# Split-float products in a Trainium2 decoder layer: the three passes of two products dealt out alternately

## The chip, the cores and the metric

The kernel runs on one core of one Trainium2 chip. The metric is the device time of one launch in microseconds (us); three runs before the change give a median of 1633.29 us (1633.14 to 1633.54). The engines are named as in the profile: PE (TensorE, matrix products; PEld is its weight load), DVE (VectorE), ACT (ScalarE), POOL (GpSimd), SP (SyncE, which issues most DMAs).

## The reference

One decoder layer on x of 1024 rows (sequence) by 1024 columns, all in float32:

```
def hybrid_mixer(h, lower_bound, w_in, conv_w, ..., w_out):
    proj = h @ w_in                                   # 1024 x 8192
    xa, ga, q, f, v, g, m_a, m_b = jnp.split(proj, SPLIT_POINTS, axis=-1)
    xa = causal_depthwise_conv(xa, conv_w, conv_b)
    y_a = rg_lru(xa, w_r, b_r, w_i, b_i, lam) * jax.nn.gelu(ga)
    ...
    o = rms_norm(hgrn2_chunkwise(qf, kf, log_f, vf), hg_norm)
    y_b = o * jax.nn.silu(g)
    y = jax.nn.sigmoid(m_a) * y_a + jax.nn.sigmoid(m_b) * y_b
    return y @ w_out

x = x + hybrid_mixer(rms_norm(x, norm_mix), ...)
h = rms_norm(x, norm_mlp)
x = x + jnp.square(jax.nn.relu(h @ w_up)) @ w_down    # 1024 x 4096 hidden
return rms_norm(x, norm_final)
```

`rg_lru` has two gate products per 256-column block (`w_r`, `w_i`) and a linear recurrence along the sequence; `hgrn2_chunkwise` is gated linear attention with 8 heads of 128.

## The kernel before

**Split products.** PE works on float32r operands, so each float32 operand is kept as a high part and a rest (`split`, L75: ACT casts the high part, L76; DVE subtracts, L77). A product is then three passes that add up in one PSUM bank: high x low, high x high, low x high (`mm3`, L113 to L117). L115, L116 and L117 in the profile are these passes; the output's name tells the product. Of the eight PSUM banks four have the tag `pj`, two `sc`, two `hg` (L59).

**Mixing stage** (two chunks c of 512 rows, four head pairs p each; L626 to L645). For every pair: `project_v` (L282) makes v with the rows as output partitions, four row tiles one after the other, each in a bank of its own and copied out by ACT (L293). `project` (L270) makes one of xa, q, f, g, mb, ga, ma: two output tiles `pp[0]` and `pp[1]` of 128 x 512 in two `pj` banks, eight contraction tiles, and for each contraction tile the three passes of `pp[0]` and then those of `pp[1]`: 48 matmuls. `rg_lru` (L326) has for each half s of the pair's channels two gate banks, `pr` (six matmuls) and then `pi` (six); ACT makes sigmoids and a tanh of them (L337 to L340), DVE a reciprocal (L345), some products and the scan (L352). Its tiles `rw`, `ri` and `rr` have one buffer each. `hgrn` (L381) is a chain on DVE: products with decays (`mul`, L384), and between them five blocks of small score matmuls on PE (`sc`: three at L394, one at L479, one at L497) that need q x f, qa, qb and kk from DVE. `gates` (L561) projects g, mb, ga, ma; DVE multiplies with `pj_g` straight out of its banks (L566), then merges g with the sigmoid of mb (L571).

**Output projection**: chunk 0 in `out_proj` (L599: four row tiles in four banks), chunk 1 inside the second norm's loop (L714 to L736: two row tiles at a time, then adds on DVE and the norm of those rows).

**MLP**, one level of a Strassen-like scheme. In the up projection (`hidden`, L804) each step fills one bank. In the down projection (L936 to L971), eight blocks kb take two quads `qs` each, and for two row tiles `pr` of a half the seven steps of `PLAN` run: for each `pr` six matmuls (three per quad) into the bank (X, Y or Z; X goes on accumulating while DVE has read its partial sum), then for each `pr` one DVE add into `x2` (L963). The first quad's tiles come from pools on the left side, the second's from pools opened with `side="right"` (L880 to L901). In the last half of the last block the row tiles run one after the other (`alone`).

**Order.** The program is written in the order above, but a scheduler of the framework orders each engine's instructions by readiness and priority (`rg_lru` and the weight splits run at raised priority), so the gate products stand inside f, the score blocks inside g, mb and ga, and the splits of coming weights anywhere on ACT and DVE. Weights come through four raw buffers (DMA from SP) and six `w` buffers, that is three tiles of high and rest (L79 to L92).

Of the kernel before, what the change touches and what calls it, by code (L numbers as in the profile page):

```python
# [18 lines left out]
P = 128  # L19
# [13 lines left out]
QUADS = 16  # L33
# [8 lines left out]
def trunk(ctx: ExitStack, tc: tile.TileContext, x, wts, mlp, pv, gains, mask_f, mask_u, out):  # L42
# [66 lines left out]
    def next_w():  # L109
        used[0] += 1  # L110
        return get_w(used[0] - 1)

    def mm3(o, ah, al, bh, bl, first, last, goes_on=False):  # L113
        how = {"skip_group_check": True} if goes_on else {}
        PE.matmul(o, ah, bl, start=first, stop=False, **how)  # L115
        PE.matmul(o, ah, bh, start=False, stop=False, **how)  # L116
        PE.matmul(o, al, bh, start=False, stop=last, **how)  # L117


    ident = const.tile([P, P], F32, tag="ident", name="ident")  # L120
# [149 lines left out]
    def project(c, name):  # L270

        pp = [bank("pj", f"pj_{name}_{s}") for s in range(2)]
        for half in range(2):
            wh, wl = next_w()
            for k in range(4):
                hh, hl = kt(hT[c], 4 * half + k)
                for s in range(2):
                    cols = slice(k * 256 + s * P, k * 256 + (s + 1) * P)
                    mm3(pp[s], wh[:, cols], wl[:, cols], hh, hl, half == 0 and k == 0, half == 1 and k == 3)
        return pp  # L280

    def project_v(c, name):  # L282
        v = mt("v", f"v_{name}", (P, 4, 256))
        w = [next_w(), next_w()]
        for tt in range(4):
            pp = bank("pj", f"pv_{name}_{tt}")
            for k in range(8):
                hh, hl = kt(hT[c], k)
                cut = slice(tt * P, (tt + 1) * P)
                cols = slice((k % 4) * 256, (k % 4 + 1) * 256)  # L290
                wh, wl = w[k // 4]
                mm3(pp[:, :256], hh[:, cut], hl[:, cut], wh[:, cols], wl[:, cols], k == 0, k == 7)
            A.copy(v[:, tt, :], pp[:, :256])  # L293
        return v

    def conv(c, p, pp):
# [29 lines left out]
    def rg_lru(c, p, xc, xh, xl):  # L326
        wh, wl = next_w()
        hs = mt("h", f"h{c}{p}", (P, 2, T))
        for s in range(2):
            u = 2 * p + s  # L330
            pr, pi = bank("pj", f"pr{c}{u}"), bank("pj", f"pi{c}{u}")
            for o, k0 in ((pr, 0), (pi, 2)):
                for k in range(2):
                    cols = slice((k0 + k) * 256 + s * P, (k0 + k) * 256 + (s + 1) * P)
                    mm3(o, wh[:, cols], wl[:, cols], xh[:, k, :], xl[:, k, :], k == 0, k == 1)
            w = mt("rw", f"rw{c}{u}")
            A.activation(w, pr, AF.Sigmoid, bias=pvt[:, PV_BR + u : PV_BR + u + 1])  # L337
            A.activation(w, w, AF.Tanh, scale=sp4[:, u : u + 1])
# [260 lines left out]
    def out_proj(c, ys, res, done, between=lambda: None):  # L599
        for hf in range(2):  # L600
            pp = [bank("pj", f"po{c}{hf}{tt}") for tt in range(4)]
            for j in range(4):
                wh, wl = next_w()
                for k in range(2):
                    ku = 2 * j + k
                    yh, yl = kt(ys, ku)
                    cols = slice(k * 512, (k + 1) * 512)
                    for tt in range(4):
                        cut = slice(tt * P, (tt + 1) * P)
# [16 lines left out]
    for c in range(NC):  # L626
# [4 lines left out]
            out_proj(0, ys, res0, done0, lambda: first_norm(1))  # L631
        ys = a2_set(a2y, f"y{c}")
        for p in range(NPAIR):
            v = project_v(c, f"{c}{p}")
# [79 lines left out]
    for part in range(2):  # L714
# [5 lines left out]
        for hf in range(2):  # L720
            pp = {tt: bank("pj", f"po1{hf}{tt}") for tt in tts}
            for j in range(4):
                wh, wl = next_w()
                for k in range(2):
                    ku = 2 * j + k
                    yh, yl = kt(ys, ku)
                    cols = slice(k * 512, (k + 1) * 512)
                    for tt in tts:
                        cut = slice(tt * P, (tt + 1) * P)
                        mm3(pp[tt], yh[:, cut], yl[:, cut], wh[:, cols], wl[:, cols], ku == 0, ku == 7)  # L730
# [11 lines left out]
    ops_w, raw_q = {}, {}  # L742
# [193 lines left out]
    for kb in range(n_kb):  # L936
        last = kb + 1 == n_kb
        qs = order[2 * kb : 2 * kb + 2]
        for half in range(2):
# [109 lines left out]
```

## Time and profile before

| what | value |
|---|---|
| median of three runs | 1633.29 us |
| profiled execution, span from first to last instruction | 1630.3 us |
| PE busy | 1585.8 us (97%), 9240 matmuls |
| DVE busy | 1211.9 us (74%) |
| ACT busy | 762.2 us (47%) |
| mean granted TensorE clock | 0.996 of full speed |
| mixing stage of a pair | about 107 us; up projection about 320 us; down projection about 310 us |

The span is that of the profiled execution itself; what a run takes beyond it lies before the first and after the last instruction. In a group or timeline row stand the line, the engine, the operation, output<-inputs, shapes, and busy time; brackets hold the idle time of the engine just ahead of it and what ended it. Matmuls are pipelined: a row's duration is longer than the distance to the next row, so the pace of PE is read from starts.

### The profile page before, as it was taken

Reading aid. Unit: us, or ns where it says so; the run is one execution under the profiler, and the core shown is the slowest. Engines: PE = TensorE matmul, PEld = TensorE weight load, DVE = VectorE, ACT = ScalarE, POOL = GpSimd, SP = SyncE. Lnnn points to the kernel's source line nnn. Section 1 sums busy time; section 2 is a strip of 40 time slices with the busy share of each in tenths; the row PEclk is TensorE's granted clock in tenths of the full one; section 3 lists DMA queues with packets and bytes.
Section 4 is the critical chain, followed back from the end, with each engine's and each line's share of the span. In section 5 each row is a group of like instructions: output and inputs, shape, how many; then the busy total and the mean of one; then the engine's idle time right before and its main releaser. Section 6 shows DMA issues by size and latency. Waiting matters only on the chain.

```text
span 1630.3 us, 23190 instructions
## 1 busy us (share of the span) xinstructions
PE 1585.8 (97%) x9240; PEld 1303.6 (80%) x9240; DVE 1211.9 (74%) x1751; ACT 762.2 (47%) x1186; POOL 62.8 (4%) x99
## 2 busy tenths in 40 slices
PE   7999999999999999999999998999999999999998
PEld 6788788788788788788787876888888878888886
DVE  5975956848764965848759688977777888888876
ACT  4643545435442544436435566767766732221113
POOL 0010100100100000000100000000000000000000
PEclk9999999999999999999999998999999999999999
DMA  6222223223244222222222352666666566666652
GB/s 236 91 66 91 91 66 103 66 91 93 78 165 142 80 77 91 78 84 98 66 91 91 125 200 102 262 247 239 233 248 247 216 259 237 238 246 249 252 207 104
DMA packets 57996, 246.51 MB, mean 151 GB/s; under 512 B 6688, under 2 KB 6816, under 8 KB 47136
## 3 DMA queue, kind: packets, MB, share of 16 engines
q1 hardware_dynamic: 56304, 239.27, 40.8%
q10 hardware_dynamic: 1584, 5.77, 1.0%
q8 instruction: 72, 1.18, 0.3%
q14 instruction: 36, 0.29, 0.1%
HBM read 185.24 MB, written 59.77 MB: 150 GB/s over the span
## 4 chain that ended last, share of the span: by engine, by line
PE 82%; DVE 15%; issue 1%; ACT 1%; DMA 1%; POOL 0%; DVEq 0%; POOLq 0%; SPq 0%; ACTq 0%
PE dX L115 4%; PE dX L117 4%; PE dX L116 4%; PE uX L115 3%; PE uX L117 3%; PE uX L116 3%; DVE wL L77 2%; PE pj_ga L117 2%; PE pj_ga L116 2%; PE pj_ga L115 2%; PE pj_ma L117 2%; PE pv L116 2%; PE pv L115 2%; PE pj_ma L116 2%; PE pv L117 2%; PE pj_f L117 2%
## 5 line engine op out<-in xcount | busy, mean ns | idle before, releaser
L77 DVE TENSOR_TENSOR wL<-raw,wH 128x1024 fp32r<-128x1024 f32 x160 | 194.4, 1215 | 151.3 <-ACT wH L76 148.7
L76 ACT CAST wH<-raw 128x1024 fp32r<-128x1024 f32 x160 | 167.9, 1050 | 166.9 <-issue 67.1
L963 DVE TENSOR_TENSOR acc<-acc,dX 128x512 f32<-128x512 f32 x128 | 86.7, 682 | 29.6 <-PE dX L117 28.9
L76 ACT CAST wA<-q 128x512 fp32r<-128x512 f32 x32 | 19.8, 621 | 130.9 <-PE dX L117 82.8
L963 DVE TENSOR_TENSOR acc<-acc,dY 128x512 f32<-128x512 f32 x64 | 43.6, 683 | 16.6 <-PE dY L117 14.9
L345 DVE RECIPROCAL rr<-rr 128x512 f32<-128x512 f32 x16 | 53.5, 3345 | 0.0
L823 ACT ACTIVATE b<-b 128x512 f32<-128x512 f32 x48 | 30.2, 631 | 38.7 <-DVE b L822 38.6
L115 PE MATMUL pv<-wL,hT0H 128*128 128x256 f32 x128 | 37.1, 289 | 0.0
L117 PE MATMUL pv<-wH,hT0L 128*128 128x256 f32 x128 | 36.7, 286 | 0.0
L116 PE MATMUL pv<-wH,hT0H 128*128 128x256 f32 x128 | 36.6, 286 | 0.0
L115 PE MATMUL pv<-wL,hT1H 128*128 128x256 f32 x128 | 36.5, 285 | 0.0
L116 PE MATMUL pv<-wH,hT1H 128*128 128x256 f32 x128 | 36.2, 283 | 0.0
L117 PE MATMUL pv<-wH,hT1L 128*128 128x256 f32 x128 | 36.2, 283 | 0.0
L311 DVE SCALAR_TENSOR_TENSOR xc<-xp,pvt,xc 128x512 f32<-128x512 f32 x48 | 33.1, 746 | 0.0
L551 ACT ACTIVATE on<-po 128x128 f32<-128x128 f32 x64 | 17.0, 278 | 33.5 <-PE po L541 33.2
L570 ACT ACTIVATE smb<-pj_mb 128x512 f32<-128x512 f32 x16 | 9.6, 597 | 45.4 <-PE pj_mb L117 45.2
L824 ACT ACTIVATE b<-b 128x512 f32<-128x512 f32 x48 | 30.0, 629 | 1.1
L384 DVE TENSOR_TENSOR seg<-seg 128x128 f32<-128x128 f32 (+2 forms) x96 | 26.8, 309 | 0.2
L565 ACT ACTIVATE g<-pj_g 128x512 f32<-128x512 f32 x16 | 9.6, 598 | 37.2 <-PE pj_g L117 37.2
L444 POOL TENSOR_SCALAR seg<-seg 128x128 f32<-128x128 f32 (+1 forms) x16 | 12.6, 790 | 360.9 <-DVE seg L384 360.9
L117 PE MATMUL pj_ga<-hT1H,wL 128*128 128x512 f32 x64 | 26.5, 414 | 0.0
L115 PE MATMUL uX<-h2B11L,wA 128*128 128x512 f32 x64 | 26.2, 409 | 0.3 <-DVE rstd_h L137 0.3
(1854 smaller groups left out, 5258.3 us busy)
## 6 DMA issues: line engine op xcount, KB each, us to landing
raw<-wts_in SPq DMA_DIRECT2D x160, 512.0 KB, 3.5
q<-mlp_in SPq DMA_DIRECT2D x64, 512.0 KB, 4.0
x<-x_in SPq DMA_DIRECT2D x8, 512.0 KB, 5.6
acc<-x ACTq DMA_DIRECT2D x8, 512.0 KB, 6.0
y_out<-acc SPq DMA_DIRECT2D x16, 256.0 KB, 2.1
xs<-x_in SPq DMA_DIRECT2D x8, 256.0 KB, 4.2
x<-xs SPq DMA_DIRECT2D x8, 256.0 KB, 2.1
x2s<-x_in SPq DMA_DIRECT2D x4, 512.0 KB, 4.8
```

The costliest lines, as they stand in the source:

```text
L76: keep(A.copy(h, src))
L77: keep(V.tensor_tensor(out=lo, in0=src, in1=h.bitcast(F32), op=ALU.subtract))
L115: PE.matmul(o, ah, bl, start=first, stop=False, **how)
L116: PE.matmul(o, ah, bh, start=False, stop=False, **how)
L117: PE.matmul(o, al, bh, start=False, stop=last, **how)
L311: V.scalar_tensor_tensor(xc[:, s, :], xp[:, j : j + T], pvt[:, PV_CW + 8 * j + u : PV_CW + 8 * j + u + 1], xc[:, s, :], op0=ALU.mult, op1= ...
L345: V.reciprocal(rec, rec)
L384: mul = lambda o, a, b: V.tensor_tensor(out=o, in0=a, in1=b, op=ALU.mult)
L551: A.activation(on[:, 4 * s + n, :], po[:, n * P : (n + 1) * P], AF.Square, accum_out=ssq[:, 4 * s + n : 4 * s + n + 1])
L823: A.activation(b[:, at, :], b[:, at, :], AF.Relu, scale=-1.0 if at == 2 else 1.0)
L824: A.activation(b[:, at, :], b[:, at, :], AF.Square)
L963: V.tensor_tensor(out=dst, in0=dst, in1=banks[bk, pr], op=op)
```

## The change

`mm3` becomes a case of `mm3s`, which takes several products and issues the first pass of all of them, then the second of all, then the third of all. Each caller that had two products with a shared operand passes both: `project` its two output tiles, `project_v` two row tiles (except in the very first pair, which keeps one), `rg_lru` the gates `pr` and `pi` of one contraction tile, the output projections two row tiles, and the down projection the two row tiles of a step for one quad. The two products lie in different PSUM banks. The up projection still passes one product. In the down projection the quad loop is now the outer one: both row tiles with the first quad, then both with the second.

```
+    def mm3s(many, first, last, goes_on=False):
+        how = {"skip_group_check": True} if goes_on else {}
+        for o, ah, al, bh, bl in many:
+            PE.matmul(o, ah, bl, start=first, stop=False, **how)
+        for o, ah, al, bh, bl in many:
+            PE.matmul(o, ah, bh, start=False, stop=False, **how)
+        for o, ah, al, bh, bl in many:
+            PE.matmul(o, al, bh, start=False, stop=last, **how)
+
     def mm3(o, ah, al, bh, bl, first, last, goes_on=False):
-        how = {"skip_group_check": True} if goes_on else {}
-        PE.matmul(o, ah, bl, start=first, stop=False, **how)
-        PE.matmul(o, ah, bh, start=False, stop=False, **how)
-        PE.matmul(o, al, bh, start=False, stop=last, **how)
+        mm3s([(o, ah, al, bh, bl)], first, last, goes_on)
...
-                for s in range(2):
-                    cols = slice(k * 256 + s * P, k * 256 + (s + 1) * P)
-                    mm3(pp[s], wh[:, cols], wl[:, cols], hh, hl, half == 0 and k == 0, half == 1 and k == 3)
+                cols = [slice(k * 256 + s * P, k * 256 + (s + 1) * P) for s in range(2)]
+                mm3s(
+                    [(pp[s], wh[:, cols[s]], wl[:, cols[s]], hh, hl) for s in range(2)],
+                    half == 0 and k == 0,
+                    half == 1 and k == 3,
+                )
...
-        for tt in range(4):
-            pp = bank("pj", f"pv_{name}_{tt}")
+        for tts in ((0,), (1,), (2,), (3,)) if first else ((0, 1), (2, 3)):
+            pp = [bank("pj", f"pv_{name}_{tt}")[:, :256] for tt in tts]
...
-            A.copy(v[:, tt, :], pp[:, :256])
+            for i, tt in enumerate(tts):
+                A.copy(v[:, tt, :], pp[i])
...
-            for o, k0 in ((pr, 0), (pi, 2)):
-                for k in range(2):
-                    cols = slice((k0 + k) * 256 + s * P, (k0 + k) * 256 + (s + 1) * P)
-                    mm3(o, wh[:, cols], wl[:, cols], xh[:, k, :], xl[:, k, :], k == 0, k == 1)
+            for k in range(2):
+                cols = [slice((k0 + k) * 256 + s * P, (k0 + k) * 256 + (s + 1) * P) for k0 in (0, 2)]
+                mm3s(
+                    [(o, wh[:, cols[i]], wl[:, cols[i]], xh[:, k, :], xl[:, k, :]) for i, o in enumerate((pr, pi))],
+                    k == 0,
+                    k == 1,
+                )
...
-                    for tt in tts:
-                        cut = slice(tt * P, (tt + 1) * P)
-                        mm3(pp[tt], yh[:, cut], yl[:, cut], wh[:, cols], wl[:, cols], ku == 0, ku == 7)
+                    cut = {tt: slice(tt * P, (tt + 1) * P) for tt in tts}
+                    mm3s(
+                        [(pp[tt], yh[:, cut[tt]], yl[:, cut[tt]], wh[:, cols], wl[:, cols]) for tt in tts],
+                        ku == 0,
+                        ku == 7,
+                    )
...
-                for pr in prs:
-                    first = (bk, pr) not in banks
-                    if first:
-                        banks[bk, pr] = bank(BANK[bk], f"d{bk}{kb}{pr}")
-                    cut = slice(pr * P, (pr + 1) * P)
-                    for i, q in enumerate(qs):
-                        wh, wl = ops_w[QUADS + q][wo]
-                        uh, ul = u_ops[q][uo]
-                        mm3(banks[bk, pr], uh[:, cut], ul[:, cut], wh, wl, first and i == 0, i == 1, not first)
+                first = (bk, prs[0]) not in banks
+                if first:
+                    banks.update({(bk, pr): bank(BANK[bk], f"d{bk}{kb}{pr}") for pr in prs})
+                cut = {pr: slice(pr * P, (pr + 1) * P) for pr in prs}
+                for i, q in enumerate(qs):
+                    wh, wl = ops_w[QUADS + q][wo]
+                    uh, ul = u_ops[q][uo]
+                    mm3s(
+                        [(banks[bk, pr], uh[:, cut[pr]], ul[:, cut[pr]], wh, wl) for pr in prs],
+                        first and i == 0,
+                        i == 1,
+                        not first,
+                    )
```

What the scheduler makes of it is shown at three places, all in the second pair of the first chunk. Line numbers of the changed kernel differ: its passes are L116, L118 and L120. A number behind a name counts buffers.

PE, the gate products inside the projection of f; before, from the first row of the gate bank `pr02` to the first of `pi02` (`pj_f01_0` and `pj_f01_1` are f's two banks):

```order
L115 MATMUL pr02_1551<-xcL01_1400,wH25_1475 128x512
L116 MATMUL pr02_1551<-xcH01_1399,wH25_1475 128x512
L117 MATMUL pj_f01_1_1472<-hT0H0_106,wL23_1408 128x512
L115 MATMUL pj_f01_0_1471<-hT0L0_108,wH23_1407 128x512
L116 MATMUL pj_f01_0_1471<-hT0H0_106,wH23_1407 128x512
L117 MATMUL pr02_1551<-xcH01_1399,wL25_1476 128x512
L115 MATMUL pr02_1551<-xcL01_1400,wH25_1475 128x512
L116 MATMUL pr02_1551<-xcH01_1399,wH25_1475 128x512
L117 MATMUL pr02_1551<-xcH01_1399,wL25_1476 128x512
L115 MATMUL pi02_1552<-xcL01_1400,wH25_1475 128x512
```

The same gates in the changed order:

```order
L116 MATMUL pr02_1551<-xcL01_1400,wH25_1475 128x512
L118 MATMUL pr02_1551<-xcH01_1399,wH25_1475 128x512
L120 MATMUL pr02_1551<-xcH01_1399,wL25_1476 128x512
L116 MATMUL pi02_1552<-xcL01_1400,wH25_1475 128x512
L118 MATMUL pi02_1552<-xcH01_1399,wH25_1475 128x512
L120 MATMUL pi02_1552<-xcH01_1399,wL25_1476 128x512
L116 MATMUL pr02_1551<-xcL01_1400,wH25_1475 128x512
L116 MATMUL pi02_1552<-xcL01_1400,wH25_1475 128x512
L118 MATMUL pr02_1551<-xcH01_1399,wH25_1475 128x512
L118 MATMUL pi02_1552<-xcH01_1399,wH25_1475 128x512
L120 MATMUL pr02_1551<-xcH01_1399,wL25_1476 128x512
L120 MATMUL pi02_1552<-xcH01_1399,wL25_1476 128x512
```

The last row of `pr02` stood ahead of all of `pi02`; now it is the last but one of the twelve of both banks, and the three rows of f that stood between them have gone ahead.

PE, the first score block `sc1_01` of the pair; before it stood inside the last passes of g:

```order
L115 MATMUL pj_g01_1_1858<-hT0L1_109,wH27_1546 128x512
L116 MATMUL pj_g01_1_1858<-hT0H1_107,wH27_1546 128x512
L394 MATMUL sc1_01_1613<-q101_1465,kk01_1534 32x48 x32
L117 MATMUL pj_g01_1_1858<-hT0H1_107,wL27_1547 128x512
L115 MATMUL pj_mb01_0_1924<-hT0L0_108,wH28_1861 128x512
```

Now it stands inside mb, and all of g is ahead of it:

```order
L120 MATMUL pj_mb01_1_1925<-hT0H0_106,wL28_1862 128x512
L116 MATMUL pj_mb01_0_1924<-hT0L0_108,wH28_1861 128x512
L116 MATMUL pj_mb01_1_1925<-hT0L0_108,wH28_1861 128x512
L411 MATMUL sc1_01_1613<-q101_1465,kk01_1534 32x48 x32
L118 MATMUL pj_mb01_0_1924<-hT0H0_106,wH28_1861 128x512
L118 MATMUL pj_mb01_1_1925<-hT0H0_106,wH28_1861 128x512
```

The block (32 matmuls in a row) has moved 15 projection matmuls further back.

DVE, from the second half's scan (`h01`) to the multiply `q101` that the first score block needs; `wL29` and `wL30` are rests of coming weight tiles (`split`). Before:

```order
L352 SCALAR_TENSOR_TENSOR h01_1550<-rr03_1601,hcar_101,ri03_1598 128x512
L77 TENSOR_TENSOR wL29_1892<-raw29_1889,wH29_1891 128x1024
L376 TENSOR_SCALAR f01_1533<-f01_1533,par_98 128x512
L377 TENSOR_SCALAR kk01_1534<-kk01_1534,par_98 128x512
L378 TENSOR_SCALAR f01_1533<-f01_1533 128x1024
L384 TENSOR_TENSOR q101_1465<-q101_1465,f01_1533 128x512
```

Now:

```order
L77 TENSOR_TENSOR wL29_1892<-raw29_1889,wH29_1891 128x1024
L369 SCALAR_TENSOR_TENSOR h01_1550<-rr03_1601,hcar_101,ri03_1598 128x512
L394 TENSOR_SCALAR kk01_1534<-kk01_1534,par_98 128x512
L393 TENSOR_SCALAR f01_1533<-f01_1533,par_98 128x512
L394 TENSOR_SCALAR kk01_1534<-kk01_1534,par_98 128x512
L395 TENSOR_SCALAR f01_1533<-f01_1533 128x1024
L77 TENSOR_TENSOR wL30_1929<-raw30_1926,wH30_1928 128x1024
L401 TENSOR_TENSOR q101_1465<-q101_1465,f01_1533 128x512
```

The split of `wL29` has moved ahead of the scan, and the split of `wL30`, which came behind the q multiply, stands ahead of it. Where the second half begins, just behind the first half's scan, DVE had the two short operations on `rw` (L342, L344) and then the multiply of `ri` (L347); now that multiply comes first.

More of the change, by code (lines that the diff above doesn't have):

```diff
@@ L276, in project, with project_v @@
                 hh, hl = kt(hT[c], 4 * half + k)
-                for s in range(2):
-                    cols = slice(k * 256 + s * P, k * 256 + (s + 1) * P)
-                    mm3(pp[s], wh[:, cols], wl[:, cols], hh, hl, half == 0 and k == 0, half == 1 and k == 3)
+                cols = [slice(k * 256 + s * P, k * 256 + (s + 1) * P) for s in range(2)]
[4 more added lines that the diff above has]
+                )
         return pp
-    def project_v(c, name):
+    def project_v(c, name, first):
         v = mt("v", f"v_{name}", (P, 4, 256))
         w = [next_w(), next_w()]
-        for tt in range(4):
-            pp = bank("pj", f"pv_{name}_{tt}")
+        for tts in ((0,), (1,), (2,), (3,)) if first else ((0, 1), (2, 3)):
+            pp = [bank("pj", f"pv_{name}_{tt}")[:, :256] for tt in tts]
+            cut = [slice(tt * P, (tt + 1) * P) for tt in tts]
             for k in range(8):
                 hh, hl = kt(hT[c], k)
-                cut = slice(tt * P, (tt + 1) * P)
                 cols = slice((k % 4) * 256, (k % 4 + 1) * 256)
                 wh, wl = w[k // 4]
-                mm3(pp[:, :256], hh[:, cut], hl[:, cut], wh[:, cols], wl[:, cols], k == 0, k == 7)
-            A.copy(v[:, tt, :], pp[:, :256])
+                mm3s(
+                    [(pp[i], hh[:, cut[i]], hl[:, cut[i]], wh[:, cols], wl[:, cols]) for i in range(len(tts))],
+                    k == 0,
+                    k == 7,
+                )
+            for i, tt in enumerate(tts):
+                A.copy(v[:, tt, :], pp[i])
         return v
@@ L331, in rg_lru @@
             pr, pi = bank("pj", f"pr{c}{u}"), bank("pj", f"pi{c}{u}")
-            for o, k0 in ((pr, 0), (pi, 2)):
-                for k in range(2):
-                    cols = slice((k0 + k) * 256 + s * P, (k0 + k) * 256 + (s + 1) * P)
-                    mm3(o, wh[:, cols], wl[:, cols], xh[:, k, :], xl[:, k, :], k == 0, k == 1)
+            for k in range(2):
+                cols = [slice((k0 + k) * 256 + s * P, (k0 + k) * 256 + (s + 1) * P) for k0 in (0, 2)]
+                mm3s(
+                    [(o, wh[:, cols[i]], wl[:, cols[i]], xh[:, k, :], xl[:, k, :]) for i, o in enumerate((pr, pi))],
+                    k == 0,
+                    k == 1,
+                )
             w = mt("rw", f"rw{c}{u}")
@@ L607, in out_proj @@
                     cols = slice(k * 512, (k + 1) * 512)
-                    for tt in range(4):
-                        cut = slice(tt * P, (tt + 1) * P)
-                        mm3(pp[tt], yh[:, cut], yl[:, cut], wh[:, cols], wl[:, cols], ku == 0, ku == 7)
+                    for tts in ((0, 1), (2, 3)):
+                        cut = {tt: slice(tt * P, (tt + 1) * P) for tt in tts}
[4 more added lines that the diff above has]
+                        )
             for tt in range(4):
@@ L633, in trunk @@
         for p in range(NPAIR):
-            v = project_v(c, f"{c}{p}")
+            v = project_v(c, f"{c}{p}", c == 0 and p == 0)
             px = project(c, f"xa{c}{p}")
@@ L727, in trunk @@
                     cols = slice(k * 512, (k + 1) * 512)
-                    for tt in tts:
-                        cut = slice(tt * P, (tt + 1) * P)
-                        mm3(pp[tt], yh[:, cut], yl[:, cut], wh[:, cols], wl[:, cols], ku == 0, ku == 7)
+                    cut = {tt: slice(tt * P, (tt + 1) * P) for tt in tts}
+                    mm3s(
+                        [(pp[tt], yh[:, cut[tt]], yl[:, cut[tt]], wh[:, cols], wl[:, cols]) for tt in tts],
+                        ku == 0,
+                        ku == 7,
+                    )
             for tt in tts:
@@ L950, in trunk @@
             ]:
-                for pr in prs:
-                    first = (bk, pr) not in banks
-                    if first:
-                        banks[bk, pr] = bank(BANK[bk], f"d{bk}{kb}{pr}")
-                    cut = slice(pr * P, (pr + 1) * P)
-                    for i, q in enumerate(qs):
-                        wh, wl = ops_w[QUADS + q][wo]
-                        uh, ul = u_ops[q][uo]
-                        mm3(banks[bk, pr], uh[:, cut], ul[:, cut], wh, wl, first and i == 0, i == 1, not first)
+                first = (bk, prs[0]) not in banks
[5 more added lines that the diff above has]
+                    uh, ul = u_ops[q][uo]
+                    mm3s(
+                        [(banks[bk, pr], uh[:, cut[pr]], ul[:, cut[pr]], wh, wl) for pr in prs],
+                        first and i == 0,
+                        i == 1,
+                        not first,
+                    )
                 for pr in prs:
```

## The prediction

> **What bounds the kernel now.** I read the page first: span, busy shares, and the group of the down projection's adds.
>
> ```profile
> span 1630.3 us, 23190 instructions
> ...
> PE 1585.8 (97%) x9240; PEld 1303.6 (80%) x9240; DVE 1211.9 (74%) x1751; ACT 762.2 (47%) x1186; POOL 62.8 (4%) x99
> ...
> L963 DVE TENSOR_TENSOR acc<-acc,dX 128x512 f32<-128x512 f32 x128 | 86.7, 682 | 29.6 <-PE dX L117 28.9
> ```
>
> TensorE (PE) is the bound; every matmul has its own weight load (9240 of each), so another order saves or adds no load. Two things can move the end: the spacing of matmuls, and the few places where PE waits for VectorE (DVE). PE's waits (total us, number, longest):
>
> ```profile
> PE xT_h L704 <- DVE rstd_h L137: 5.7, 2, 5.3
> ...
> PE sc L394 <- DVE qb L384: 5.0, 8, 0.6
> PE sc L394 <- DVE q L384: 4.0, 8, 0.5
> ```
>
> The last two come once for each of the 8 head pairs (2 chunks of 4). Such an idle time is counted from the modelled end of a matmul, so what a wait costs is better read from starts. In the timeline, the two score blocks of the second pair that show it, each with the matmul ahead of it:
>
> ```profile
> 186.91 0.39 PE L116 MATMUL pj_g<-hT0H,wH 128*128 128x512 f32 x1
> 187.79 0.89 PE L394 MATMUL sc<-q,kk 128*32 128x48 f32 x64 [0.49 <-DVE q L384]
> ...
> 196.76 0.39 PE L117 MATMUL pj_mb<-hT0H,wL 128*128 128x512 f32 x1
> 197.78 0.89 PE L394 MATMUL sc<-qb,kk 128*32 128x48 f32 x64 [0.63 <-DVE qb L384]
> ```
>
> Start to start 0.88 and 1.02 us, where a projection's matmul takes 0.227 (next part): 0.65 + 0.79 = 1.4 us lost per pair, 11.5 over 8.
>
> **The neighbour's bank: no term.** In a projection L115, L116, L117 go to one bank and the next L115 to the other; in `pv`, all to one.
>
> ```profile
> 700.22 0.39 PE L115 MATMUL pj_ma<-hT1L,wH 128*128 128x512 f32 x1
> 700.45 0.39 PE L116 MATMUL pj_ma<-hT1H,wH 128*128 128x512 f32 x1
> 700.67 0.39 PE L117 MATMUL pj_ma<-hT1H,wL 128*128 128x512 f32 x1
> 700.90 0.39 PE L115 MATMUL pj_ma<-hT1L,wH 128*128 128x512 f32 x1
> ...
> 126.83 0.28 PE L115 MATMUL pv<-wL,hT0H 128*128 128x256 f32 x1
> 126.95 0.28 PE L116 MATMUL pv<-wH,hT0H 128*128 128x256 f32 x1
> ```
>
> Two steps within a bank take 0.45 us (0.225 each), the step to the other bank 0.23, the three 0.68 (0.227 each): a neighbour in another bank gains nothing. Counted in the built orders, 1470 of the steps between neighbouring split products change bank before and 5119 after: 3649 steps change kind. The rows resolve 0.01 us over three steps; I take 0, and 1 ns either way as bounds: ±3.6 us. [...]
>
> **The gates' first bank is done later: about +4.0 us.** The scheduler rebuilds the mixing stage around the new order. Of the gate products of the second pair, here are the first matmul of f and the last of the first `pr`:
>
> ```profile
> 159.78 0.39 PE L115 MATMUL pj_f<-hT0L,wH 128*128 128x512 f32 x1
> ...
> 162.97 0.40 PE L117 MATMUL pr<-xcH,wL 128*128 128x512 f32 x1
> ```
>
> That `pr` is the 14th from the start of f (3.19 us for 13 steps, 0.23 with the slower ones among them left in). In the changed order it is the 23rd: 12 of f, then 11 of the 12 of both banks. Nine steps of 0.23 make 2.1 us. Now ACT can read `pr` while PE runs the six of `pi`; after, both banks end one matmul apart. (The Trainium skill, page Perfetto Trace Analysis, section Optimizing Tensor Performance, Matmuls: independent groups should rotate through the banks so that the evacuation of one overlaps the next group's matmuls. It speaks against this change at just this place, and the rows agree that the overlap is there now.)
>
> Behind the gates DVE is a nearly closed chain, from the recurrence to the last score operand. From the timelines of ACT and DVE: `ri` for the second half; the first half's scan and what follows it; a weight split; a merge of gates:
>
> ```profile
> 174.74 0.68 ACT L340 ACTIVATE ri<-pi,pvt 128x512 f32<-128x512 f32 x1
> ...
> 173.42 1.28 DVE L352 TENSOR_TENSOR_SCAN h<-rr,hcar,ri 128x512 f32<-128x512 f32 x1
> 174.87 0.43 DVE L342 TENSOR_SCALAR rw<-rw 128x512 f32<-128x512 f32 x1 [0.17 <-ACT rw L338]
> ...
> 184.19 1.20 DVE L77 TENSOR_TENSOR wL<-raw,wH 128x1024 fp32r<-128x1024 f32 x1
> ...
> 207.33 1.22 DVE L571 TENSOR_TENSOR g<-g,smb 128x1024 f32<-128x1024 f32 x1
> ```
>
> Between the halves DVE waits 0.17 us. Before, two short operations on `rw` (0.43 us) come first and cover the arrival of `ri`; in the changed order the multiply of `ri` comes first. `ri` has one buffer, free at the scan's end (174.70), and ACT needs 0.68 to fill it: DVE waits 0.7 to 0.8, about 0.6 more. And one more weight split stands ahead of the q multiply: 1.2 us. So q is ready 2.1 + 0.6 + 1.2 = 3.9 us later. PE's first score block stands later too: behind 47 matmuls of g before, behind 48 of g and 14 of mb now, 15 x 0.227 = 3.4 us. The wait there grows by 0.5 us. From there to the last score block PE's work grows from 54 to 58 projection matmuls (+0.9), and DVE gets the merge of g (1.2) ahead of that block's operands: even, within 0.3. I take +0.5 us per pair, 8 x 0.5 = +4.0 us. Bounds: if q is only the 2.1 us late, PE's 3.4 covers 1.3 us of waiting (-10.4 in all); or each pair loses 0.5 more (rival a), +8.0.
>
> **Norm stage: +0.5 us.** A pair of output-projection banks now ends one matmul apart, not three; its two adds on DVE have the shape of L963, 0.68 us each, and the norm behind them is what PE waits for (5.3 us at its longest). They start two steps of 0.23 later, exposed once. Were it hidden 0; on both waits 0.9.
>
> **Down projection: -1.2 us.** Six matmuls of one bank (three for each of two quads, the second quad's tiles in pools opened on the right side), and six of the up projection, whose moving tiles `hop` all lie on the right:
>
> ```profile
> 1400.64 0.39 PE L115 MATMUL dX<-ws318L,u2n 128*128 128x512 f32 x1
> ...
> 1402.03 0.39 PE L115 MATMUL dY<-ws318L,u2B 128*128 128x512 f32 x1
> ...
> 1151.34 0.40 PE L115 MATMUL uX<-h2B11L,wA 128*128 128x512 f32 x1
> ...
> 1152.74 0.40 PE L115 MATMUL uX<-h2B11L,wA 128*128 128x512 f32 x1
> ```
>
> Six take 1.39 us in the first and 1.40 in the second (0.233 each); six of a projection take 1.36. Three of each kind would make 1.38, so the two changes of side in a cycle seem to cost 0.013 us. The change cuts the changes of side from 419 to 239 (counted in the orders): 180 x 0.0065 = 1.2 us less. Bounds: 0, if the 0.013 is rounding; -2.7, if all 0.03 above 1.36 come from changing sides.
>
> Beside this, the first of two banks ends five matmuls (1.15 us) later, so its add starts later, and the bank is next written 13 matmuls (3.0 us) after, where it was 18. Two adds of 0.68 and a split of 1.2 fit into 3.0; and it is DVE that waits for PE there now (28.9 us in total, L963), so it isn't behind. I take 0; with the cover gone, a split's 1.2 us less that slack at a few of the 49 steps with splits, +3 at most. v's copies come in twos and are read only by the pair's last products: 0. The up projection keeps its order.
>
> Sum: +4.0 + 0.5 - 1.2 + 0 = +3.3 us on the span of 1630.3. The median of 1633.29 lies 3.0 us above that span, for start and end, which stay: 1636.6 us. A measurement here can tell about 0.2%, 3.3 us, from no change; the forecast sits on that bound.
>
> **Rivals.** (a) Slower: the wait moves to pj_ga. Both its banks are needed by its second matmul, one step after the first; before, the second bank only three steps after. They are pj_g's banks, freed by DVE's two multiplies with `pj_g` inside the late chain. If the chain's 0.5 us shows again there, each pair loses 0.5 more: +4.0, 1640.6 us. It decides once the second multiply ends later than the first ga matmul starts. For it: the chain is closed. Against: time lost at ga is time that DVE gains for the next block. (b) Lateness and later placing cancel: +0.5 - 1.2, 1632.6 us. For it: 3.4 and 3.9 are close. (c) Faster: q is only 2.1 us late and PE finds its operands: -10.4 + 0.5 - 1.2, 1622.2 us. Against: the extra split is in the order. (d) A bank change itself saves: a 256-column matmul of `pv` starts every 0.12 us, so 2 x 120 - 227 = 13 ns of a matmul don't depend on its length; if the 3649 steps lost them, 47 us go: 1586 us. Against: the bank changes there are now take 0.23. That the scheduler undoes the dealing is excluded by the 5119 changes.
>
> **How the numbers follow.** Forecast 0.48, (a) 0.30, (b) 0.13, (c) 0.06, (d) 0.03. The forecast's own spread, 1634 to 1639, lies half on each side of 1636.6. Slower by over 0.2%: half of it and most of (a) less its lower tail, 0.47; within: the other half, (b) and a little of (a), 0.42; faster 0.11. The range leaves out (c), (d) and the tails: 1629.0 (the bank's -3.6 on (b)) to 1644.0 (nearly +3.6 on (a)).
>
> **What would show it.** Right: 0.22 to 0.24 us between starts whatever the bank; the first gate's last matmul about 2 us later after f's start; the q multiply 3 to 5 us later; waits at the score blocks 0.5 us longer per pair; six down matmuls of one side in a row. Wrong: projection matmuls at another pace (the bank matters), the waits gone (c), or PE held at pj_ga by 0.5 us or more (a).

## The result, and the profile after

| | before | after |
|---|---|---|
| median | 1633.41 us (4 runs, 1633.14 to 1635.76) | 1640.93 us (4 runs, 1638.18 to 1642.76) |
| ratio of the times | | 1.0044, 95% interval 1.0029 to 1.0058 |
| span of the profiled execution | 1630.3 us | 1638.5 us |

The change makes the kernel 0.44% slower, 7.5 us where 3.3 were forecast. The sign of the forecast (1636.6 us) holds and the time lies inside the range, but, as the rest shows, the parts are not the ones forecast. The profiled execution after took 1640.18 us, 1.7 us beyond its span, and the other executions of the changed kernel lie as far beyond theirs. The 3.0 us that the prediction added for start and end therefore held over 1 us of the spread between executions.

The page of the changed kernel, first its totals, then the group of the down projection's adds:

```profile
span 1638.5 us, 23207 instructions
...
PE 1591.7 (97%) x9240; PEld 1302.0 (79%) x9240; DVE 1208.2 (74%) x1751; ACT 758.9 (46%) x1186; POOL 90.2 (6%) x99
...
L991 DVE TENSOR_TENSOR acc<-acc,dX 128x512 f32<-128x512 f32 x128 | 82.7, 683 | 34.7 <-PE dX L120 34.6
```

The 9240 matmuls are the same; what has grown is waiting. PE's busy time is 5.9 us longer all the same: a row lasts 0.39 us where the pace is 0.23, so the first part of a wait counts as busy, and what a wait costs is read from starts. PE's waits after (total us, number, longest):

```profile
PE sc L411 <- DVE seg L401: 4.4, 8, 0.6
PE sc L411 <- DVE q L401: 3.0, 8, 0.4
...
PE pk L542 <- DVE kk L401: 1.1, 1, 1.1
...
PE dX L116 <- DMA u3n<-u3n: 0.6, 1, 0.6
PE dX L116 <- DMA u9n<-u9n: 0.5, 1, 0.5
PE dX L116 <- DMA u11n<-u11n: 0.5, 1, 0.5
...
PE pv L116 <- DVE xs L634: 0.5, 1, 0.5
```

The waits at the score blocks, which were forecast to grow by 4 us, have shrunk from 9.0 to 7.4. New are waits for a DMA in the down projection, one at `pk` and two at `pv` (the second, on `v`, 0.3 us). Where the 8.2 us of the span arise is read by comparing the starts of the same matmul in both timelines:

| first matmul of | before | after | later by |
|---|---|---|---|
| pv of chunk 0, fourth pair | 341.42 | 341.51 | 0.09 |
| the first output projection | 449.26 | 450.51 | 1.25 |
| xa of chunk 1, first pair | 508.47 | 511.80 | 3.33 |
| the second output projection | 926.94 | 930.83 | 3.89 |
| the ninth quad of the up projection | 1151.34 | 1155.26 | 3.92 |
| down projection, second block | 1349.16 | 1352.99 | 3.83 |
| down projection, eighth block | 1582.87 | 1591.08 | 8.21 |

Seven pairs together bring 0.6 us, the last pair of chunk 0 1.2, the passage between the chunks 2.1, the down projection 4.4.

**Down projection.** In its second to seventh block the first half grows by 0.46, 0.90, 1.15, 0.96, 0.95 and 0.81 us, and each second half shrinks by 0.14 (19.51 to 19.37). The third block, PE's timeline before and after around the odd quad's n2 tile, `u3n`:

```profile
1396.27 0.39 PE L117 MATMUL dZ<-wA1219H,u3B 128*128 128x512 f32 x1
1396.50 0.39 PE L115 MATMUL dX<-ws119L,u3n 128*128 128x512 f32 x1
```

```profile
1399.37 0.40 PE L116 MATMUL dZ<-wA1218L,u2B 128*128 128x512 f32 x1
1400.34 0.73 PE L116 MATMUL dX<-ws119L,u3n 128*128 128x512 f32 x2 [0.58 <-DMA u3n<-u3n]
```

And the reload's row in the view of that tile, before and after (the last figure: us from issue to landing):

```profile
L897 SPq DMA_DIRECT2D u3n<-u3n x1: 427/427/427, 1388.0 to 1388.0; - x1
...
DMA to landing us min/median/max: 7.6/7.6/7.6
```

```profile
L921 SPq DMA_DIRECT2D u3n<-u3n x1: 433/433/433, 1391.5 to 1391.5; - x1
...
DMA to landing us min/median/max: 8.8/8.8/8.8
```

Before, the tile lands at 1395.6 and is read at 1396.5, 8.3 us into the block (which begins at 1388.17): 0.9 us to spare. After, it lands at 1400.3; PE has only one matmul of dZ between the even quad's n2 products and the odd quad's, where it had six, and is there 7.3 us into the block (1392.32), before the tile is.

Two things add up. PE arrives 1.0 us earlier in the block while the reload is issued only 0.7 us earlier; this alone would have left some 0.5 us to spare. The reload itself takes 1.2 us longer, and that makes PE wait. It is so throughout: the five tiles u3n to u11n take 8.7 to 9.0 us in place of 6.8 to 7.6, and the even quad's n2 tiles, 6.6 to 7.1 in place of 4.7 to 5.5, are read within 0.15 us of their landing. With the longest reload times of before they would land, by this estimate, 6.8 us (odd) and 4.3 us (even) into the block, ahead of PE at 7.1 and 5.5. The regrouping made the margin smaller; why the reloads became slower is open.

**Passage between the chunks.** Of the 2.1 us, 0.7 arise inside the first output projection (its first matmul is 1.25 us late, the first of v 1.96) and 1.4 inside v, whose row tiles now need two banks at once. DVE's add that frees the fourth bank of the first output projection waits for a tile of x, and PE for the add:

```profile
505.55 1.29 DVE L634 TENSOR_TENSOR xs<-po,xs 128x512 f32<-128x512 f32 x2 [5.04 <-DMA xs<-x_in]
```

```profile
504.42 0.40 PE L120 MATMUL pv<-wH,hT1L 128*128 128x256 f32 x2
505.17 0.38 PE L116 MATMUL pv<-wL,hT1H 128*128 128x256 f32 x1 [0.35 <-ACT v L307]
...
506.30 0.39 PE L116 MATMUL pv<-wL,hT1H 128*128 128x256 f32 x1 [0.51 <-DVE xs L634]
```

**Last pair of chunk 0.** On DVE the norm of the next chunk stands ahead of the last `kk`; it waits for POOL, and all behind it waits too:

```profile
427.04 1.28 DVE L145 SCALAR_TENSOR_TENSOR xn<-x,rstd_x,gain 128x1024 f32<-128x1024 f32 x1 [1.52 <-POOL rstd_x L144]
428.24 1.22 DVE L77 TENSOR_TENSOR wL<-raw,wH 128x1024 fp32r<-128x1024 f32 x1
429.38 0.69 DVE L401 TENSOR_TENSOR kk<-kk,seg 128x512 f32<-128x512 f32 x1
```

```profile
430.12 0.66 PE L542 MATMUL pk<-ident,kk 128*128 128x128 f32 x4 [1.05 <-DVE kk L401]
```

Before, the same `xn` stood behind that `kk` and cost nothing.

### The profile page after: what moved, and what is told of

Its sections match the earlier page's. It is cut to its first block, busy times and chain, and to the rows that moved or that the text cites. A ratio compares the mean times of both kernels' runs of the same rounds, so it can differ in the third digit from the quotient of the medians.

```text
span 1638.5 us, 23207 instructions
## 1 busy us (share of the span) xinstructions
PE 1591.7 (97%) x9240; PEld 1302.0 (79%) x9240; DVE 1208.2 (74%) x1751; ACT 758.9 (46%) x1186; POOL 90.2 (6%) x99
## 4 chain that ended last, share of the span: by engine, by line
PE 73%; DVE 15%; DMA 5%; ACT 4%; issue 2%; POOL 1%; SPq 0%; DVEq 0%; POOLq 0%; ACTq 0%
DVE wL L77 3%; PE uX L120 3%; PE uX L116 3%; PE uX L118 3%; PE dX L116 3%; PE dX L118 3%; PE dX L120 3%; PE pj_xa L116 2%; PE pj_ma L120 2%; PE pj_ma L116 2%; PE pj_xa L118 2%; PE pj_xa L120 2%; PE pj_ma L118 2%; PE pj_q L120 2%; PE pj_q L116 2%
## 5 line engine op out<-in xcount | busy, mean ns | idle before, releaser
L483 POOL TENSOR_SCALAR scT<-dd 32x256 f32<-32x256 f32 x32 | 46.9, 1464 | 45.6 <-DVE dd L455 44.1
L364 DVE TENSOR_TENSOR ri<-ri,xc 128x512 f32<-128x512 f32 x16 | 11.1, 692 | 35.0 <-ACT ri L357 35.0
L354 ACT ACTIVATE rw<-pr,pvt 128x512 f32<-128x512 f32 x16 | 11.0, 690 | 45.6 <-PE pr L120 30.9
L116 PE MATMUL pv<-wL,hT0H 128*128 128x256 f32 x128 | 30.0, 295 | 0.0
L120 PE MATMUL pv<-wH,hT0L 128*128 128x256 f32 x128 | 29.4, 291 | 0.0
L118 PE MATMUL pv<-wH,hT0H 128*128 128x256 f32 x128 | 29.4, 291 | 0.0
L401 DVE TENSOR_TENSOR kk<-kk,seg 128x768 f32<-128x768 f32 (+1 forms) x32 | 27.8, 869 | 0.0
L116 PE MATMUL pv<-wL,hT1H 128*128 128x256 f32 x128 | 26.4, 286 | 0.9 <-DVE xs L634 0.5
L77 DVE TENSOR_TENSOR wA<-q,wA 128x512 fp32r<-128x512 f32 x32 | 22.0, 687 | 5.5 <-ACT wA L76 5.4
L116 PE MATMUL uX<-h2B11L,wA 128*128 128x512 f32 x64 | 26.0, 406 | 0.0
L118 PE MATMUL pv<-wH,hT1H 128*128 128x256 f32 x128 | 25.9, 283 | 0.0
```

Source lines behind the costliest of these rows:

```text
L77: keep(V.tensor_tensor(out=lo, in0=src, in1=h.bitcast(F32), op=ALU.subtract))
L401: mul = lambda o, a, b: V.tensor_tensor(out=o, in0=a, in1=b, op=ALU.mult)
L483: G.tensor_scalar(scT[32 * b : 32 * b + 32, :, 32 * b : 32 * b + 32], dd[32 * b : 32 * b + 32, :, :], 1.0, 0.0, op0=ALU.mult, op1=ALU.add,)
```

## The experiments

Each of the twelve kernels is the kernel before with some of the six dealt places (project, project_v, rg_lru, the two output projections, the down loop), or the changed kernel with an edit. Ratios are to the kernel before, with their 95% intervals. A trace shows one execution, which can lie some 3 us from the median of its kernel.

| kernel | dealt alternately | median us | ratio |
|---|---|---|---|
| down_old | all but the down loop | 1637.81 | 1.0032 (1.0020 to 1.0045) |
| down_only | down loop | 1635.51 | 1.0014 (1.0005 to 1.0023) |
| gates_only | gates of rg_lru | 1630.04 | 0.9984 (0.9976 to 0.9993) |
| early_n | all, n2 loaded earlier | 1636.94 | 1.0030 (1.0018 to 1.0042) |
| down_swap | all, steps swapped | 1640.27 | 1.0049 (1.0037 to 1.0062) |
| proj_only | project | 1631.02 | 0.9993 (0.9985 to 1.0002) |
| out_pv_only | v and output projections | 1634.71 | 1.0010 (1.0001 to 1.0019) |
| gates_down_swap | gates, down loop, swapped | 1633.14 | 1.0006 (0.9996 to 1.0015) |
| gates_proj | gates, project | 1635.49 | 1.0016 (1.0007 to 1.0025) |
| down_swap1 | down loop, swapped after the first block | 1632.60 | 1.0002 (0.9993 to 1.0012) |
| gates_down_swap1 | gates and the same down loop | 1630.82 | 0.9990 (0.9981 to 0.9999) |
| gates_down_rev | gates, down loop, n2 earlier and read later | 1629.41 | 0.9976 (0.9967 to 0.9985) |

**The down loop put back (down_old), and alone (down_only).** The loop of the old order, in the changed kernel's words:

```
+                for pr in prs:
+                    for i, q in enumerate(qs):
+                        mm3(banks[bk, pr], uh[:, cut], ul[:, cut], wh, wl, first and i == 0, i == 1, not first)
-                for i, q in enumerate(qs):
-                    mm3s([(banks[bk, pr], ...) for pr in prs], first and i == 0, i == 1, not first)
```

> The changed kernel with the down projection's loop put back to the old order (quads inside, one row tile after the other); all else dealt alternately. Theory A, read from the changed kernel's trace: in six of its eight blocks PE waits for the reload of the odd quad's n2 tile, and the first half of the block grows by 0.5 to 1.15 us, while every undisturbed half gains 0.14; together the down projection costs 4.2 us. Then this kernel takes 1640.9 - 4.2 = 1636.7 us, the waits on u3n to u11n are gone, and the halves take 19.4 to 19.5 us as before. Theory B, the terms as predicted (gates +4.0, norm +0.5, down -1.2): the down loop is a gain, and without it the time is 1642.1 us.

> The kernel before with only the down projection's loop in the new order (quads outside, two row tiles dealt alternately). Theory A (the reload of the odd quad's n2 tile comes too late): 1633.4 + 4.2 = 1637.6 us, with PE waiting on a u tile's DMA once in most blocks. Theory B (only fewer changes of side): 1633.4 - 1.2 = 1632.2 us and no such wait.

Measured 1637.8 and 1635.5: putting the loop back saves 3.1 us, putting it in alone costs 2.2. The sign is theory A's, the size three quarters of its 4.2 us in the first and half of it in the second. In both directions the term that was forecast as a gain of 1.2 us is a loss. In down_only the waits on u tiles are fewer (u9n 0.6, u8n 0.4, u5n and u0n 0.2), and they stand where a reload is slow: u9n takes 9.3 us, while u3n takes 7.4 and is not waited for.

**The gates alone (gates_only).** Only the loop of rg_lru in the new form (pr and pi of one contraction tile together).

> The kernel before with only the gate products of rg_lru dealt alternately. The predicted term (gate bank done 2 us later, q multiply 3.9 us later against 3.4 us of later placing, 0.5 us per pair) gives 1633.4 + 4.0 = 1637.4 us, with the first score block's wait 0.5 us longer in each pair. Theory A (the scheduler places the score blocks as late as their operands are, 0.1 us per pair): 1633.4 + 0.6 = 1634.0 us, waits at the score blocks as before.

Measured 1630.0 us, 0.16% faster than before, where the predicted term says 4 slower: both theories fail. The trace shows why: in the pair that the prediction looked at, DVE's q multiply and PE's first score block, first before (the block's own row stands in the prediction), then with the gates alone:

```profile
186.88 0.86 DVE L384 TENSOR_TENSOR q<-q,f 128x512 f32<-128x512 f32 x1
```

```profile
190.05 0.85 DVE L393 TENSOR_TENSOR q<-q,f 128x512 f32<-128x512 f32 x1
```

```profile
190.70 0.39 PE L116 MATMUL pj_mb<-hT0L,wH 128*128 128x512 f32 x1
191.02 0.89 PE L403 MATMUL sc<-q,kk 128*32 128x48 f32 x64
```

From the first matmul of f (159.78 before, 159.48 with the gates alone) the multiply begins 27.10 us later before and 30.57 now: 3.5 more. But the scheduler has moved the block behind 17 more projection matmuls and all of f and g stand ahead: PE reaches it with 0.09 us lost (start to start 0.32 against 0.23) where it lost 0.65. Over the five score blocks of this pair PE loses 1.66 us in place of 2.19, and the pair takes 107.17 in place of 107.50. The chain on DVE is later, and PE comes later still.

**The reload moved ahead in SP's queue (early_n).**

```
-                for i in range(2):
-                    load_u(order[2 * kb + 2 + i], *side[i][1:])
+                for i, groups in ((0, U_GROUPS[:3]), (1, U_GROUPS), (0, U_GROUPS[3:])):
+                    load_u(order[2 * kb + 2 + i], *side[i][1:], groups)
```

> The changed kernel with the odd quad's n2/T3 tile loaded ahead of the even quad's in SP's queue, not behind it: its buffer has been free some 8 us by then, and only the in-order queue holds it back; its issue comes about 3.2 us earlier. Theory A1 (the queue position makes it late): the waits on u3n to u11n are gone, the down projection loses the 6.2 us of waits and keeps its 2.1 us of gain: 1640.9 - 6.2 = 1634.7 us. Rival A2 (the transfers themselves are slow in the new order, or another tile's reload is as late): the wait moves to the even quad's n2 tile or stays, and the time stays above 1639 us.

Measured 1636.9: 4.0 us below the changed kernel and 2.2 above theory A1's 1634.7. The intervals of the two kernels overlap a little; in the traces the down projection from its second to its eighth block is 4.1 us shorter. SP's timeline of the two kernels, first the changed one, then this:

```profile
1391.13 0.32 SPq L921 DMA_DIRECT2D u2n<-u2n  x1
1391.49 0.43 SPq L921 DMA_DIRECT2D u3n<-u3n  x1
```

```profile
1389.16 0.43 SPq L922 DMA_DIRECT2D u3n<-u3n  x1
1391.56 0.32 SPq L922 DMA_DIRECT2D u2n<-u2n  x1
```

u3n no longer waits behind u2n, whose buffer is freed only by one of the last products of the block ahead. The waits on u3n to u11n are gone, as theory A1 says. A smaller one is left at the even quad's n2 tile, 0.25 to 0.36 us in four blocks (start to start 0.48 to 0.59 ahead of it): rival A2's move, in small. The edit did one thing more: the scheduler now puts seven dZ matmuls ahead of the even quad's n2 products, so PE reads the odd tile 8.5 us or more into the block. The conclusion does not hang on that: the odd tiles land 3.5 to 4.9 us into the block and would have been there for the changed kernel's reader, at 7.1. That PE waits for the reload, and that an earlier place in the queue ends the wait, is shown.

**Steps swapped (down_swap, and with the gates alone gates_down_swap).**

```
-for i, plan in enumerate(PLAN)
+for i, plan in ((k, PLAN[k]) for k in (0, 1, 3, 2, 4, 5, 6))
```

> The changed kernel with the third and fourth step of the down projection swapped (the Z products ahead of the X products with n2; the sums are the same, added in another order), so that the even quad's n2 tile is read 12 matmuls (2.8 us) later in a block and the odd quad's 6 or more (1.4 us). The DMAs are issued as before. Theory A (PE reads the n2 tiles before their reload has landed): all waits on u2n to u11n and u0n are gone, the 6.2 us of them are saved, the gain of 0.14 per half stays: 1640.9 - 6.2 = 1634.7 us. Rival (the halves grow for another cause, the adds or the banks): 1639 us or more.

> The kernel before with only the gates and the down loop dealt alternately, and the down steps three and four swapped. If the parts add up: gates alone measured -3.3, the down loop without its waits saves 0.14 in each of some 15 halves, -2.1: 1633.3 - 5.4 = 1627.9 us. If the swap brings a wait of its own or the side changes save nothing without it: 1630 us or more.

Measured 1640.3 and 1633.1, 5.6 and 5.2 us above theory A and above the sum of the parts. The waits on u tiles are gone, for two reasons at once: PE reads later, and, other than expected, the odd quad's reload is also issued earlier, 10.9 us ahead of its block where it was 0.8. In down_swap the second to seventh block together are 0.9 us shorter than before, where the changed kernel's are 4.4 longer. But the first block, which reloads nothing, loses 3.9 us, and 4.6 in the other kernel. PE's waits in down_swap:

```profile
PE dZ L116 <- DVE wA1230L L77: 2.3, 1, 2.3
...
PE dX L116 <- DVE acc L991: 1.5, 2, 1.0
...
PE dY L116 <- DVE acc L991: 1.0, 1, 1.0
```

With dZ moved ahead, two steps of the X bank follow each other, and X may go on only when DVE has added its partial sum. Some 1.4 us of each loss come from a stretch at half pace (last section).

**project alone, v and the output projections alone (proj_only, out_pv_only).**

> The kernel before with only project dealt alternately (two banks of a projection end one matmul apart); gates, v, output and down projections as before. Of the changed kernel's 7.5 us, 3.0 are the down loop's and the gates alone save 3.3, so the other parts cost about 7.8 us together. Theory C (project costs them: ACT and DVE get both banks at once, and the scheduler moves the score blocks too little): 1633.3 + 5 or more, 1638 us or above, with longer waits at the score blocks. Theory D (project is neutral; v's pairs of banks and the output projection cost it, or it arises only with the gates): within 1.5 us of 1633.3. The predicted terms hold no cost for project by itself except rival (a)'s wait at pj_ga.

> The kernel before with only v (two row tiles in two banks at once) and the two output projections dealt alternately. The changed kernel's trace shows 2.1 us lost between the first output projection and the first v of the second chunk (PE waits for the residual adds that free the second bank of a pair of v). Theory D: 1633.3 + 2.1 = 1635.4 us, all of it there, nothing elsewhere. The predicted terms: 0 for v, +0.5 for the norm stage, 1633.8 us.

project alone is not told from no change (0.9985 to 1.0002), which leaves at most 0.3 us of cost: theory C falls. v and the output projections cost 0.10%, and the trace of out_pv_only puts 2.0 us between the first output projection and the first xa of chunk 1, with the waits shown above (`pv` on `xs` 0.5, on `v` 0.3) and nothing in the pairs: theory D. Of the 2.0 us, 0.6 stand ahead of v and 1.4 in it, as in the changed kernel; the two were not tried apart.

**Gates and project together (gates_proj).**

> The kernel before with the gates and project dealt alternately; v, output and down projections as before. PE's order inside a pair is then that of the changed kernel. Alone, the gates measured -3.3 us and project -2.3. Theory E (what a pair gains or loses is how far the scheduler moves the score blocks against how far their operands move; the two parts share one wait, so they don't add up): as in the changed kernel's trace, about 0.05 us per pair and 1.15 us at the pk block of the first chunk's last pair: 1633 + 1.6 = 1634.6 us. If the parts add up: 1633 - 5.6 = 1627.4 us. The term as predicted (+4.0 for the gates): 1637 us.

Measured 1635.5: the parts, about -3 and -1 to -2 alone, give +2.6 together. Theory E has the direction; in the profiled execution 1.5 us of it stand at `pk` (idle 1.4 us, 1.1 in the changed kernel) and 0.8 in the first half of the down projection's second block, which this kernel does not change. There PE waits for the reload of u0n, which took 6.6 us where it took 4.9 before. proj_only, whose down loop is the old one too, loses 0.7 and 0.5 us in the same way (u0n 6.6, u4n 6.5): in the old order, too, PE waits when a reload is this slow. Why the pairs gain nothing is seen in the changed kernel, whose pairs have the same order. ACT and PE where g begins:

```profile
176.71 0.69 ACT L357 ACTIVATE ri<-pi,pvt 128x512 f32<-128x512 f32 x1 [0.96 <-DVE h L369]
```

```profile
177.03 0.39 PE L120 MATMUL pj_g<-hT0H,wL 128*128 128x512 f32 x1
177.45 0.50 PE L116 MATMUL pj_g<-hT0L,wH 128*128 128x512 f32 x1
```

The gates stand behind 12 to 15 matmuls of f (5 to 11 with the gates alone), the second half's `ri` and scan come 1 us later, and the second bank of g is that of the last `pi`: ACT reads it until 177.40, because its own tile `ri` was held by the scan of the half before. PE loses 0.3 us there, and with the slower f and gates (0.2) this gives back the 0.45 us that the score blocks gain.

**The down loop without its waits (down_swap1, gates_down_swap1, gates_down_rev).** In the first two the swap leaves out the first block. In the third no step is swapped: the early load is kept, and the third step takes the odd quad first.

```
+            steps = range(7) if kb == 0 or alone else (0, 1, 3, 2, 4, 5, 6)
...
-                for i, q in enumerate(qs):
+                for i, q in enumerate(qs[::-1] if step == 2 and kb > 0 else qs):
```

> The kernel before with only the down loop in the new order, and its third and fourth step swapped in all blocks but the first (and not in the last half, where row tiles run one by one). The first block reloads no u tile, and the swap there brought a wait for the adds. Theory A (changes of side are what the new order saves, late n2 reloads what it costs, and the swap hides these): no wait on a u tile, the first block 0.2 us and each later half about 0.1 us shorter, 1633.0 - 1.5 = 1631.5 us; the predicted term, -1.2 (0 to -2.7), gives 1631.8. If the new order brings other waits: 1633 us or more.

> The gates and the down loop dealt alternately, the steps swapped as in the kernel beside it (not in the first block). The gates sit 700 us ahead of the down projection, so here the two should add up: -3.3 and -1.5, 1633.0 - 4.8 = 1628.2 us. Above 1630 us one of the two does not hold.

> The gates and the down loop dealt alternately, no step swapped. Instead the odd quad's n2/T3 tile is loaded ahead of the even quad's in SP's queue, and in the third step PE takes the odd quad first, so that the even quad's n2 tile is read some 7 matmuls (1.6 us) later; in the swapped order two steps of one X bank came one after the other and PE waited for the add between them (1.57 and 0.84 us in two blocks), which this order avoids. Theory A: no wait on a u tile and no new wait for the adds, each half of the down projection 0.14 us shorter, 14 halves -2.0; with the gates' -3.3: 1633.0 - 5.3 = 1627.7 us, below the gates alone (1630.0). If only the gates' gain is kept: 1630 us; if the late reload is still there: 1632 us.

down_swap1, 1632.6 us, is not told from the kernel before; its undisturbed halves are 0.05 to 0.18 us shorter, but three of its first halves take 0.21 to 0.47 more, behind a wait for the add of X. gates_down_swap1, 1630.8, misses the expected sum by 2.6. Its profiled execution is the slowest of its eleven: 1.8 us go in the first block, most of them at half pace (last section), and 2.2 in three first halves in which X follows X:

```profile
1399.86 0.63 PE L118 MATMUL dY<-ws318H,u2B 128*128 128x512 f32 x2
1401.66 0.51 PE L116 MATMUL dX<-ws318L,u2n 128*128 128x512 f32 x1 [1.17 <-DVE acc L977]
```

gates_down_rev avoids that, and has the lowest median of all: 1629.4 us, 0.24% below the kernel before and 0.7% below the changed one. Its interval and that of the gates alone overlap, so how much of its down gain is real is not settled by times. In its profiled execution each second half of the second to seventh block is 0.18 us shorter than before, the first halves between 0.18 shorter and 0.38 longer, since a wait on an even quad's tile is left in some; the first block loses 1.6 us, most of it in a stretch at half pace (last section).

## Why the prediction was right, and where it was wrong

**The neighbour's bank, no term: right.** In the changed kernel neighbouring matmuls of ma go to two banks:

```profile
703.80 0.62 PE L116 MATMUL pj_ma<-hT1L,wH 128*128 128x512 f32 x2
704.25 0.61 PE L118 MATMUL pj_ma<-hT1H,wH 128*128 128x512 f32 x2
704.70 0.62 PE L120 MATMUL pj_ma<-hT1H,wL 128*128 128x512 f32 x2
705.16 0.62 PE L116 MATMUL pj_ma<-hT1L,wH 128*128 128x512 f32 x2
```

Six starts in 1.36 us, 0.227 each, as before; the 96 matmuls of xa and q of a pair take 21.79 us in both. Rival (d) is excluded: another bank for the neighbour by itself brings nothing on this kernel.

**The gates' first bank: each link held, the difference failed.** `pr` ends 2.0 us later after f's start (164.86 less 159.67 is 5.19, against 3.19). The 2.1 forecast for it came from steps of 0.23, though its 3.19 us over 13 steps are 0.245 each; nine such steps make 2.2. DVE waits for the second `ri`, as worked out:

```profile
177.43 0.69 DVE L364 TENSOR_TENSOR ri<-ri,xc 128x512 f32<-128x512 f32 x1 [0.76 <-ACT ri L357]
...
190.60 0.86 DVE L401 TENSOR_TENSOR q<-q,f 128x512 f32<-128x512 f32 x1
191.51 0.89 PE L411 MATMUL sc<-q,kk 128*32 128x48 f32 x64 [0.40 <-DVE q L401]
```

The multiply comes 30.93 us after f's start, 3.8 later than before (forecast 3.9). The step that failed is "3.4 us later. The wait there grows by 0.5 us": PE, had it not to wait, would reach the block 3.9 us later (31.84 less the 0.56 lost, against 28.01 less 0.65), since f, the gates and the second bank of g slow it by 0.5 that the count of 15 matmuls left out. So the lost time at the block falls by 0.1, and a pair takes 107.62 in place of 107.50: seven pairs 0.6 us, not 3.5. That the two cancel was rival (b), which had 0.13. With a sign that hangs on the difference of two terms of nearly 4 us, 0.48 for the forecast was too sure; gates_only shows the same chain with the other sign.

**Rival (a) was half seen.** A dealt pair needs its second bank earlier, and PE does wait for that: 0.3 us per pair, but at g's second bank, held by `pi`, not at ga's.

**Norm stage, +0.5: wrong place.** The second norm's stage brings 0.03 us (3.89 to 3.92). The passage between the chunks, where the prediction gave v's paired banks 0 ("read only by the pair's last products"), costs 2.1, of which 1.4 in v. The prediction looked at who reads v and not at who frees the banks: the adds behind a DMA.

**Down projection, -1.2: the term was right and small beside what was left out.** Undisturbed halves shrink by 0.14; 14 of them give 2.0 us, within the bounds 0 to -2.7. That it comes from the changes of side and not from the banks was not tried by itself; it fits that gates_down_rev, where the third step begins on the side on which the second ended, gains 0.18 per half. The cover that the prediction weighed was that of the adds; the reloads from SP, 0.9 us ahead of their reader, were not looked at. Six blocks lose 5.2 us in their first halves, 6.1 with the 0.14 each that they should have gained.

**The sum.** Forecast: gates 4.0, norm 0.5, down -1.2, in all 3.3. Found in the span: pairs 0.6, last pair of chunk 0 1.2, passage 2.1, down 4.4. The forecast was right on the sign with three of its four terms wrong in sign, place or size: that the sum has the right sign and lies in the range is largely luck, since its one large term was nearly nothing and the two largest losses stood where it had a gain and a zero. What it shares with the result is that the banks bring nothing and that regrouping takes cover away.

What stays open: why the reloads take longer in the changed kernel (u3n to u11n 8.8 us on average, 8.1 in down_only, and 7.2 to 8.0 in the six profiled kernels with the old loop); what the order at `pk`, which was seen in two kernels, would cost if it alone were changed; and most of why single executions of one kernel differ by 1 to 4 us.

## What to carry to other kernels

When a change regroups a loop, list for each operand tile when its reload lands and when its first reader comes; here a margin of 0.9 us was gone when five matmuls changed places and the reload took 1.2 us longer. Two banks that end together are also two banks that must be free together: look at who frees them, not only at who reads them. A wait that is the difference of two moved chains has no sign until both are known to a tenth; and parts that share one such wait don't add up, so test them alone and together.

## What the runs showed of the hardware

After a short wait PE can fall to half pace. In gates_down_rev PE waits 1.56 us in the first block of the down projection; soon after, seven steps take 0.43 us each, and the granted clock by stretches of 3 us (columns: window, length, PE busy, instructions, granted clock, DMA share, GB/s) is:

```profile
1309.00:1312.00 3.00, 1.44 (x6) 0.94 0.99 393
1312.00:1315.00 3.00, 3.00 (x9) 0.50 1.01 426
1315.00:1318.00 3.00, 3.00 (x14) 0.99 0.50 208
```

That nearly doubles the wait's price (7 x 0.2 = 1.4 us more). It does not follow each such wait: the kernel before loses nearly as long at the same place (1.83 us start to start, idle 1.44) without it, and out_pv_only longer (2.37, idle 1.98). The Trainium skill (page TensorE: Matmul & The Clock Gate, section Part 1: The HAM clock gate) has half rate follow an idle window of about 3.4 us; here 1.95 us from start to start were enough. Such stretches behind a short wait stand in six of the fourteen profiled executions (about 1.4 us each). They can explain a part of the spread between executions: of 89 executions of the kernel before, those with a mean granted clock of 0.997 took 1632.6 us on average, those with 0.994 or 0.995 took 1633.9. The whole spread, 1630.5 to 1636.6 us, is wider than that.
